# Half of an output projection as seven quadrant products in place of eight

## The chip, the cores and the metric

The kernel runs on one core of a Trainium2 chip, as one program with one launch. The metric is the device time of a whole execution in microseconds; lower is better. Every time below comes from runs on the chip or from one execution that the hardware profiler recorded.

## The reference

The program computes a model of two layers over 512 tokens of width 1024, in float32. Layer A mixes tokens by a gated spatial product in chunks of 128 and by attention to 256 memory rows; layer B by forgetting attention and by memory attention. Each layer then projects what it mixed, adds it to the residual after a norm, and runs a feed-forward of width 2816. Of layer A, with its output projection, the following is computed:

```python
proj = a @ w_in_a[layer]
u, v, q_mem = proj[..., :768], proj[..., 768:1536], proj[..., 1536:]
main = chunked_spatial_gating(u, v, w_s, b_s, ln_g, ln_b)     # gelu(u) * (w_s @ layernorm(gelu(v)) + b_s)
mixed = concatenate([main, memory_attention(q_mem, mem_n, w_mem_kv[layer])], axis=-1)   # 512 x 1024
h = h + rmsnorm(mixed @ w_out[layer], ln_mix_post[layer])
f = rmsnorm(h, ln_ffn_pre[layer])
f = (silu(f @ w_ffn_gate[layer]) * (f @ w_ffn_up[layer])) @ w_ffn_down[layer]
h = h + rmsnorm(f, ln_ffn_post[layer])
```

The change concerns `mixed @ w_out[0]`, a 512 x 1024 by 1024 x 1024 product.

## The kernel before

*Numbers in two parts.* Every float32 operand of a product is split into a high part (a cast to fp32r, on ScalarE, L276) and a low part (the operand less its high part, on VectorE, L277); `split` issues the pair. `mm3` (L217 to L221) then makes one product of three matmuls: high by high, high by low, low by high. So a product of 128 input rows with 512 columns costs three matmuls on TensorE, and each weight tile of 128 x 512 costs one operation on ScalarE and one on VectorE.

*Blocks.* The width of 1024 is eight blocks of 128. Blocks 0 to 5 of `mixed` are the six groups of the spatial product, 6 and 7 the two pairs of memory heads. `ORDER` (L40) takes them as 6, 7, 0, 1 and then 2, 3, 4, 5, since the first four are known earlier. The projection is cut accordingly into two halves of its inputs. `out_part` (L963) does the first: for each half of the output (`dh`) and each of four token blocks (`tb`), two pieces of two input blocks each; with the second piece the sum is copied out of PSUM to `ys[tb][dh]` by ScalarE (L982). In such a product 128 tokens of `mixed` are the stationary operand and 512 columns of weights the moving one. `mix_tail`, through `tail_of` (L877), does the second half: for each token block and output half, four input blocks in twelve matmuls, then an addition of `ys` (L904), the sum of squares (L917) and, per token block, the scaling by a power that POOL computes (L290, L944).

*The stage around it.* In `layer_a`, `attend` runs the four memory heads with pieces of other work between their steps. `join` (L446) puts two heads side by side and splits them into `mixed[6]` and `mixed[7]`. Then `gate_inputs(m)` (L793) makes the m-th block of `u`: 24 matmuls, a multiplication (L797) and a gelu (L798). `stats` and `normed(j)` make the normalized value rows and their parts. `spatial(g)` (L835) makes eight short matmuls into two PSUM tiles, four VectorE operations on them (L847, L850), a product with `us[g]` (L853) and, by `store`, the split into `mixed[g]`. The order is written out by hand: three `gate_inputs`, then `spatial(m - 3)` and `gate_inputs(m)` in turn for m = 3 to 5, then `spatial(g)` for g = 3 to 5, with 5, 5 and 6 of the sixteen pieces of `out_part` behind them. `queue` puts the loading of a block of weights three pieces ahead of its use.

*What orders the instructions.* Each engine runs its own list in order. A planner makes these lists: it goes through the program with its own estimate of durations and lets each engine take, of what it holds to be ready, what stands first in the program. Buffers are counted by tag: 36 tiles of 512 columns (`act`), 4 raw weight tiles, 8 high and 8 low weight parts, 4 temporaries, 6 of tag `p`, 3 PSUM tiles each of tags `mm` and `lg`, 2 of `tr`. An instruction that needs a tile is not ready before one is free. `behind` (L262) adds an order between two instructions by hand.

*Seven products.* The feed-forwards already use a form of Strassen's scheme. For a 2 x 2 block product, sums of the input blocks and of the weight blocks are formed, and seven products, summed in different ways, replace eight. `Down` (L1174) does so for the last matrix. Some of the sums of weights are made ahead, in DRAM: `sums_ahead` (L170) takes the next entry of `to_sum`, copies a block of weights to a DRAM tile by SP's queue and lets POOL's queue add another onto it (L190). `load` (L162) calls it for every second load while `credit[0]` is 0.5 (L857).

Of the kernel before, what the change touches and what calls it, by code (L numbers as in the profile page):

```python
# [43 lines left out]
def hybrid(ctx: ExitStack, tc: tile.TileContext, i: dict, out: bass.AP):  # L44
# [125 lines left out]
    def sums_ahead():  # L170

        if not to_sum:
            return
        w, layer, m = to_sum.pop(0)
        both = two_sums[w, layer, m] = dp.tile([P, 1040], F32, tag=name("sums"), name=name("sums"))[:, :1024]
        with behind(last_load[0]):
            if w == "w_down":
                four = both.rearrange("p (m k c) -> p m k c", m=4, k=2)  # L180
                for dh in range(2):
                    nc.sync.dma_start(four[:, :, dh, :],
                                      i[w][layer, 4 * dh : 4 * dh + 4, :, m, :].rearrange("m p c -> p m c"))
                more = i[w][layer, 4:8, :, m : m + 2, :].rearrange("m p k c -> p m (k c)")
                with behind(*(last_pow if m == 2 else ())):
                    G.dma_start(both.rearrange("p (m c) -> p m c", m=4), more, accum_op=ALU.add)
            else:
                nc.sync.dma_start(both.rearrange("p (a c) -> p a c", a=2),
                                  i[w][layer, m : m + 2, :, :512].rearrange("a p c -> p a c"))
                G.dma_start(both, i[w][layer, m + 1], accum_op=ALU.add)  # L190

    def moving_pair(src, aside=False):
# [4 lines left out]
        parts = []  # L197
# [6 lines left out]
    def out_weights(layer, kp, dh, aside=False):  # L204
        return moving_pair(i["w_out"][layer, 4 * dh : 4 * dh + 4, :, 256 * kp : 256 * kp + 256]
                           .rearrange("m p c -> p m c"), aside)

# [237 lines left out]

    def join(o, mixed, m, j):  # L446


        own, _ = rows(j)
        if j == 0:  # L450
            mixed[m] = act("mixedhi"), act("mixedlo")
# [41 lines left out]
    class MemHead(Softmax):  # L493
        def __init__(self, layer, pr, j, q, dst):
            super().__init__()
            self.kv, self.pr, self.j, self.q, self.dst = mem_kv[layer], pr, j, q[pr], dst
            self.blocks = (0, 1)
# [14 lines left out]
        def values(self, b):  # L512
# [5 lines left out]
            if b == 1:  # L518
                return join(self.o, self.dst, 6 + self.pr, self.j)

# [74 lines left out]

    def mem_heads(layer, q, mixed):
        heads = [MemHead(layer, pr, j, q, mixed) for pr in range(2) for j in range(2)]
        return heads


    def layer_a():
# [106 lines left out]
        with tc.tile_pool(name="sgu", bufs=1) as lp:  # L708
# [95 lines left out]
            attend(mem_heads(0, q, mixed), between=between)  # L804
            with behind(last_exp[0], last_turn[0]):
# [29 lines left out]
            def spatial(g):  # L835
# [17 lines left out]
                V.tensor_mul(t2, t.rearrange("p a b -> p (a b)"), us[g])  # L853
# [22 lines left out]

# [86 lines left out]
    def out_part(layer, mixed):  # L963
# [22 lines left out]
        return ys, [block(dh) for dh in range(2)]  # L986

    def mix_tail(layer, mixed, ys):
        attended = last_exp[0]

        def load(kp, dh, aside):
            with behind(attended):
                return out_weights(layer, 2 + kp, dh, aside)

        return tail_of([mixed[k] for k in ORDER[4:]], load, ys)

# [812 lines left out]
```

## Time and profile before

| | us |
|---|---|
| median of 3 runs | 1082.82 |
| lowest and highest run | 1082.56, 1083.18 |
| span of the profiled execution, first to last instruction | 1081.0 |
| median of the runs less this span | 1.8 |
| TensorE busy | 1073.2 |
| VectorE busy | 942.9 |
| ScalarE busy | 736.4 |
| POOL busy | 74.4 |

The profiled execution has no time of its own beside its span; what lies around the span is taken as the difference to the median of the runs. Engines are named PE (TensorE matmuls), PEld (its weight loads, which overlap with matmuls), DVE (VectorE), ACT (ScalarE), POOL (GpSimd) and SP (the queue that issues most transfers). A row of a timeline gives the start, the duration, the engine, the line of the kernel, the operation, output <- inputs, the shape and how many follow each other; in square brackets stands the idle time in front of it and what ended that. A row of windows gives for one stretch of the span each engine's busy time with its count of instructions.

### The profile page before, as it was taken

What the parts mean: (1) busy time and instruction counts of PE and PEld (TensorE: products, weight loads), DVE (VectorE), ACT (ScalarE), POOL (GpSimd) and SP (SyncE); (2) the same over time, 40 slices, a digit from 0 to 9 for tenths busy, and PEclk for the clock granted to TensorE, in tenths of its full rate; (3) what the DMA queues carried; (4) which work ended last, traced back from release to release, by engine and by line L of the source; (5) the groups of instructions that cost most, each with busy time, mean ns of one, the idle gap of its engine ahead of it and who ended that gap; (6) DMA issues with size and microseconds to landing.
All of it is one profiled execution on the core that took longest, in us unless ns stands there. A gap on an engine that the chain in (4) does not pass through costs nothing.

```text
span 1081.0 us, 20005 instructions
## 1 busy us (share of the span) xinstructions
PE 1073.2 (99%) x7234; PEld 982.1 (91%) x7234; DVE 942.9 (87%) x1894; ACT 736.4 (68%) x1605; POOL 74.4 (7%) x99
## 2 busy tenths in 40 slices
PE   9999999999999999999999999999999999999998
PEld 7998889999999988998988998889999999988996
DVE  8889659999989999996987899959999988999975
ACT  8776468666666667576765677858766666667564
POOL 0101001000000100000110111001000000000001
PEclk9999999999999999999999999999999999999999
DMA  7556666967665967264441754445977663646332
GB/s 275 167 136 180 190 157 204 255 186 194 172 169 149 300 177 230 92 206 126 128 128 48 208 128 115 126 123 171 255 199 194 162 158 115 176 128 206 112 118 79
DMA packets 131979, 179.52 MB, mean 166 GB/s; under 512 B 9964, under 2 KB 94200, under 8 KB 131880
## 3 DMA queue, kind: packets, MB, share of 16 engines
q1 hardware_dynamic: 119608, 160.53, 48.0%
q0 software_dynamic: 11712, 17.40, 10.3%
q8 instruction: 57, 0.93, 0.4%
q14 instruction: 42, 0.34, 0.1%
q10 hardware_dynamic: 560, 0.31, 0.1%
HBM read 158.71 MB, written 43.00 MB: 187 GB/s over the span
## 4 chain that ended last, share of the span: by engine, by line
PE 96%; ACT 2%; DVE 0%; issue 0%; DMA 0%; POOL 0%; POOLq 0%; ACTq 0%
PE a L219 7%; PE a L221 7%; PE a L220 7%; PE y L219 4%; PE y L220 4%; PE y L221 4%; PE ps L219 4%; PE ps L221 4%; PE ps L220 4%; PE e L219 4%; PE e L221 4%; PE e L220 3%; PE p L221 3%; PE p L219 3%; PE p L220 3%; PE x L219 3%
## 5 line engine op out<-in xcount | busy, mean ns | idle before, releaser
L276 ACT CAST whi<-raw 128x512 fp32r<-128x512 f32 x315 | 188.0, 618 | 59.8 <-PE a L220 12.9
L277 DVE TENSOR_TENSOR wlo<-raw,whi 128x512 fp32r<-128x512 f32 x315 | 210.2, 687 | 20.0 <-ACT whi L276 17.1
L219 PE MATMUL a<-xshi,whi 128*128 128x256 f32 x480 | 135.0, 281 | 0.0
L220 PE MATMUL a<-xslo,whi 128*128 128x256 f32 x480 | 134.9, 281 | 0.0
L221 PE MATMUL a<-xshi,wlo 128*128 128x256 f32 x480 | 134.7, 281 | 0.0
L276 ACT CAST whi<-room 128x512 fp32r<-128x512 f32 x160 | 98.1, 621 | 46.5 <-PE x L220 9.6
L277 DVE TENSOR_TENSOR wlo<-room,whi 128x512 fp32r<-128x512 f32 x160 | 108.9, 687 | 7.5 <-ACT whi L276 5.3
L219 PEld LDWEIGHTS a<-xshi,whi 128*128 128x128 f32 x480 | 90.3, 188 | 1.1 <-ACT e L1166 0.3
L220 PEld LDWEIGHTS a<-xslo,whi 128*128 128x128 f32 x480 | 90.4, 188 | 0.7
L221 PEld LDWEIGHTS a<-xshi,wlo 128*128 128x128 f32 x480 | 90.5, 189 | 0.0
L219 PE MATMUL ps<-xshi,whi 128*128 128x256 f32 x192 | 55.0, 289 | 0.1
L220 PE MATMUL ps<-xslo,whi 128*128 128x256 f32 x192 | 54.1, 283 | 0.0
L221 PE MATMUL ps<-xshi,wlo 128*128 128x256 f32 x192 | 54.0, 282 | 0.0
L276 ACT CAST ff<-u 128x256 fp32r<-128x256 f32 x80 | 32.3, 407 | 29.1 <-PE p L221 15.5
L219 PE MATMUL y<-whi,mixedhi 128*128 128x512 f32 x128 | 51.2, 400 | 0.0
L221 PE MATMUL p<-whi,ff 128*128 128x512 f32 x128 | 50.5, 395 | 0.0
L219 PE MATMUL p<-whi,ff 128*128 128x512 f32 x128 | 50.5, 395 | 0.0
L220 PE MATMUL y<-wlo,mixedhi 128*128 128x512 f32 x128 | 50.5, 395 | 0.0
L221 PE MATMUL y<-whi,mixedlo 128*128 128x512 f32 x128 | 50.4, 394 | 0.0
L220 PE MATMUL p<-wlo,ff 128*128 128x512 f32 x128 | 50.3, 393 | 0.0
L219 PE MATMUL x<-xshi,whi 128*128 128x256 f32 x160 | 45.1, 282 | 0.0
L220 PE MATMUL x<-xslo,whi 128*128 128x256 f32 x160 | 45.1, 282 | 0.0
(391 smaller groups left out, 3575.6 us busy)
## 6 DMA issues: line engine op xcount, KB each, us to landing
room<-in_w_up SPq DMA_DIRECT2D x36, 512.0 KB, 4.0
raw<-in_w_gate SPq DMA_DIRECT2D x24, 512.0 KB, 4.1
raw<-in_w_down SPq DMA_DIRECT2D x20, 512.0 KB, 4.5
sums<-in_w_gate SPq DMA_DIRECT2D x16, 512.0 KB, 5.8
sums<-in_w_gate POOLq DMA_DIRECT2D x16, 512.0 KB, 5.9
raw<-in_w_out SPq DMA_DIRECT2D x16, 512.0 KB, 3.5
sums<-in_w_down SPq DMA_DIRECT2D x32, 256.0 KB, 5.6
sums<-in_w_down POOLq DMA_DIRECT2D x16, 512.0 KB, 7.8
```

What stands on the lines that cost most here:

```text
L219: PE.matmul(o, w[0], x[0], start=start, stop=False, skip_group_check=more)
L220: PE.matmul(o, w[0], x[1], start=False, stop=False, skip_group_check=more)
L221: return PE.matmul(o, w[1], x[0], start=False, stop=stop, skip_group_check=more)
L276: last_hi[0] = A.copy(hi, src)
L277: last_split[0] = last_hi[0], (eng or V).tensor_sub(lo, src, hi)
```

## The change

The first half of layer A's projection is computed by a new class `OutPairs`, for two pairs `q` of input blocks: (6, 7) and (0, 1). In each pair, the inputs are two blocks by two halves of the tokens, and the weights two blocks by two halves of the output.

- `join` and `spatial` no longer split blocks 6, 7, 0 and 1: they hand them over whole (`pairs.whole`).
- `form` makes, per pair, sums of the four input quadrants (four VectorE operations of 256 columns) and their parts (three full splits and a half one).
- Per pair, two of the sums of weights are formed in DRAM by `sums_ahead`, which gets a branch for `w_out`, called twice among the memory heads. Two more are formed on VectorE (products 3 and 5).
- `pieces` runs products 0, 2, 3, 1, 4, 6, 5, each for both pairs, each with two token tiles of three matmuls. Their weights are split three pieces ahead. `tap` takes the running sums out of PSUM.
- Ten of the fourteen pieces (products 0, 2, 3, 1, 4) run 4, 2 and 4 behind the last three `spatial`; four (products 6, 5) run ahead of the tail's third token block.
- The second output half comes out with its sign turned in `ys`, which the tail undoes by subtracting.
- The tail's weights of layer A are loaded in two loads of 256 KB each into `act` tiles in place of one of 512 KB into a raw tile (`apart`).
- The eight gate sums of the feed-forward that were paced by loads (`credit[0] = 0.5`) are now called from `gate_inputs(1)` to `(5)` and from the last three `spatial`.

The core of the diff:

```diff
@@ sums_ahead
+            if w == "w_out":
+                four = both.rearrange("p (m k c) -> p m k c", m=4, k=2)
+                c = slice(256 * m, 256 * m + 128)
+                for dh in range(2):
+                    nc.sync.dma_start(four[:, :, dh, :],
+                                      i[w][layer, 4 * dh : 4 * dh + 4, :, c].rearrange("m p c -> p m c"))
+                more = i[w][layer, 4:8, :, 256 * m : 256 * m + 256].rearrange("m p c -> p m c")
+                G.dma_start(both.rearrange("p (m c) -> p m c", m=4), more, accum_op=ALU.add)
@@ moving_pair
+        if apart:
+            raws = [act("raw", F32).rearrange("p (m c) -> p m c", m=4) for _ in range(2)]
+            for x in range(2):
+                load(raws[x], src[:, :, x * P : x * P + P])
...
@@ join
-            return lambda: split(joined[m], *mixed[m])
+            return (lambda: whole(m, joined[m])) if whole else lambda: split(joined[m], *mixed[m])
@@ layer_a
             def gate_inputs(m):
                 gate_weights(m + 2)
+                if m:
+                    sums_ahead()
...
+            to_sum.extend(("w_out", 0, q) for q in range(2))
+            pairs = OutPairs(0)
+            between[1].append(sums_ahead)
+            between[2].append(sums_ahead)
...
-                store(t2, mixed, g)
+                if g < 2:
+                    pairs.whole(g, t2)
+                else:
+                    store(t2, mixed, g)
...
-            credit[0] = 0.5
...
-            ys, outs = out_part(0, mixed)
-            more = queue(outs)
             for m in range(3, NG):
                 spatial(m - 3)
                 gate_inputs(m)
+                if m == 3:
+                    pairs.forms(6)
+                elif m == 4:
+                    pairs.load_first()
+                    pairs.forms(0)
+            pairs.load_more()
+            begin, more = pairs.pieces()
+            begin()
             for g in range(3, NG):
                 spatial(g)
-                for f in take(more, 5 if g < NG - 1 else 6):
+                sums_ahead()
+                for f in take(more, 2 if g == 4 else 4):
                     f()
-        return mix_tail(0, mixed, ys)
+        tail, ys, tail_split = mix_tail(0, mixed, pairs.ys)
+
+        def mixed_tail(tb, *rest):
+            if tb == 2:
+                for f in more:
+                    f()
+            return tail(tb, *rest)
+
+        return mixed_tail, ys, tail_split
@@ OutPairs
+        ORDERED = (0, 2, 3, 1, 4, 6, 5)
...
+        def form(self, u0, u1):
+            t = temp("tsum")
+            one = act("mixedhi"), act("mixedlo")
+            split(u1, *one)
+            V.tensor_sub(t[:, left], u1[:, right], u0[:, right])
+            V.tensor_sub(u0[:, right], u0[:, left], u0[:, right])
+            V.scalar_tensor_tensor(out=t[:, right], in0=u0[:, right], scalar=-1.0, in1=u1[:, right],
+                                   op0=ALU.mult, op1=ALU.subtract)
+            zero = act("mixedhi"), act("mixedlo")
+            split(u0, *zero)
+            V.scalar_tensor_tensor(out=u1[:, left], in0=t[:, right], scalar=-1.0, in1=u1[:, left],
+                                   op0=ALU.mult, op1=ALU.subtract)
+            both, last = (flat(p()), flat(p())), p()
+            split(t, *both)
+            split(u1[:, left], last[:, 0], last[:, 1])
...
+        def weights(self, n, q):
+            r = self.raws[q]
+            if n == 3:
+                V.tensor_add(r["a11"], r["a21"], r["a11"])
+            elif n == 5:
+                V.tensor_add(r["a12"], r["a11"], r["a12"])
+            src = r[{0: "a11", 1: "s3", 2: "a12", 3: "a11", 4: "a22", 5: "a12", 6: "a21"}[n]]
+            w = pair_of_parts()
+            split(src, *(x.rearrange("p (m c) -> p m c", c=P) for x in w))
+            return w
+
+        def product(self, n, q, w):
+            bank = {0: "x", 3: "x", 6: "x", 5: "x", 2: "z", 1: "y", 4: "y"}[n]
+            first = n in (0, 2, 1)
+            if first and q == 0:
+                self.o[bank] = [ps("tr" if bank == "x" else "lg", s="y") for _ in range(2)]
+            for t in range(2):
+                x = self.pairs[q][n]
+                tokens = slice(t * P, (t + 1) * P)
+                mm3(self.o[bank][t], tuple(part[:, tokens] for part in x), w, first and q == 0, False, True)
+                if q:
+                    self.tap(n, t, self.o[bank][t])
+
+        def tap(self, n, t, o):
+            if n in (0, 3, 1):
+                kept = self.o[n, t] = act("kept", F32)
+                A.copy(kept, o)
+            elif n == 5:
+                ys[2 + t][0] = plain("y")
+                A.copy(ys[2 + t][0], o)
+            else:
+                tb, dh, of = {2: (t, 0, 0), 4: (t, 1, 3), 6: (2 + t, 1, 1)}[n]
+                ys[tb][dh] = plain("y")
+                V.tensor_add(ys[tb][dh], o, self.o[of, t])
+
+        def pieces(self):
+            order = [(n, q) for n in self.ORDERED for q in range(2)]
...
+            def run(x):
+                if x + 3 < len(order):
+                    ready[x + 3] = self.weights(*order[x + 3])
+                self.product(*order[x], ready.pop(x))
```

More of the change, by code (lines that the diff above doesn't have):

```diff
@@ L190, in sums_ahead, with moving_pair @@
                 G.dma_start(both, i[w][layer, m + 1], accum_op=ALU.add)
-    def moving_pair(src, aside=False):
+    def moving_pair(src, aside=False, apart=False):
+        parts = []
+        if apart:
+            raws = [act("raw", F32).rearrange("p (m c) -> p m c", m=4) for _ in range(2)]
+            for x in range(2):
+                load(raws[x], src[:, :, x * P : x * P + P])
+            for raw in raws:
+                hi, lo = (t.rearrange("p (m c) -> p m c", m=4) for t in pair_of_parts(aside=aside))
+                split(raw, hi, lo)
+                parts.append((hi, lo))
+            return parts
         raw = wp.tile([P, 1024], F32, tag="raw", name=name("raw"), bufs=4)
@@ L444, in hybrid, with join @@
     joined = {}
-    def join(o, mixed, m, j):
+    def join(o, mixed, m, j, whole=None):
         own, _ = rows(j)
         if j == 0:
-            mixed[m] = act("mixedhi"), act("mixedlo")
+            mixed[m] = None if whole else (act("mixedhi"), act("mixedlo"))
             f = joined[m] = temp("f", tag="acc", bufs=2)
@@ L493, in hybrid, with __init__ @@
     class MemHead(Softmax):
-        def __init__(self, layer, pr, j, q, dst):
+        def __init__(self, layer, pr, j, q, dst, whole):
             super().__init__()
+            self.whole = whole
             self.kv, self.pr, self.j, self.q, self.dst = mem_kv[layer], pr, j, q[pr], dst
@@ L594, in attend, with mem_heads @@
             f()
-    def mem_heads(layer, q, mixed):
-        heads = [MemHead(layer, pr, j, q, mixed) for pr in range(2) for j in range(2)]
+    def mem_heads(layer, q, mixed, whole=None):
+        heads = [MemHead(layer, pr, j, q, mixed, whole) for pr in range(2) for j in range(2)]
         return heads
@@ L803, in layer_a @@
             between[4] = [lambda k=k: gate_piece(k) for k in range(KT)]
-            attend(mem_heads(0, q, mixed), between=between)
+            attend(mem_heads(0, q, mixed, pairs.whole), between=between)
             with behind(last_exp[0], last_turn[0]):
@@ L992, in load @@
             with behind(attended):
-                return out_weights(layer, 2 + kp, dh, aside)
-        return tail_of([mixed[k] for k in ORDER[4:]], load, ys)
+                return out_weights(layer, 2 + kp, dh, aside, layer == 0)
+        return tail_of([mixed[k] for k in ORDER[4:]], load, ys, turned_sign=layer == 0)
     def boundary(phase, post, pre, nnorm, dst, block, evac, scaled=None):
```

44 lines of the change are left out of this document (39 added, 5 removed).

## The prediction

> **What bounds the kernel now.** I read the head of the page first, then the chain of waits, then tables of windows around the place of the change, and last the timelines of TensorE and VectorE inside them.
>
> ```profile
> span 1081.0 us, 20005 instructions
> PE 1073.2 (99%) x7234; PEld 982.1 (91%) x7234; DVE 942.9 (87%) x1894; ACT 736.4 (68%) x1605; POOL 74.4 (7%) x99
> PEclk9999999999999999999999999999999999999999
> PE 96%; ACT 2%; DVE 0%; issue 0%; DMA 0%; POOL 0%; POOLq 0%; ACTq 0%
> ```
>
> TensorE (PE) is 99% busy at full granted clock and is 96% of the chain that ended last. A matmul taken away anywhere is worth its own spacing, as long as what feeds the next ones keeps up. VectorE (DVE), at 87%, is the engine most likely not to.
>
> The change lies between the last softmax of layer A's memory heads, at about 83 us, and the end of the projection's tail, at about 163 us. The columns after the length of a stretch are busy times, with instruction counts in brackets, then clock, DMA share and GB/s.
>
> ```profile
> core 0: us, PE busy (x) PEld busy (x) DVE busy (x) ACT busy (x) POOL busy (x), PEclk, DMA share, GB/s
> 83.20:138.90 55.70, 55.70 (x266) 46.16 (x265) 44.79 (x92) 31.62 (x58) 5.45 (x6) 1.00 0.70 180
> 138.90:163.00 24.10, 24.10 (x115) 19.87 (x114) 11.44 (x22) 13.84 (x32) 2.49 (x4) 1.00 0.52 152
> 89.60:107.00 17.40, 17.40 (x85) 14.46 (x84) 16.92 (x34) 11.91 (x22) 0.87 (x1) 1.00 0.68 176
> ```
>
> TensorE has no idle time in any of these. VectorE has 55.7 - 44.8 = 10.9 us of room before the tail starts and 24.1 - 11.4 = 12.7 us within it, but it is not spread evenly: from 89.6 to 107 us it is 97% busy (16.92 of 17.40). So the stage has one saturated engine, and a second one that is saturated in its first third.
>
> **The change, part by part.** *TensorE.* The first half of the projection is now 2 halves of the output x 4 token blocks x 4 input blocks x 3 matmuls = 96 matmuls of 512 columns. Seven products x 2 pairs of input blocks x 2 token tiles x 3 = 84. What one costs is its spacing, not its duration, since they overlap:
>
> ```profile
> 130.49 0.47 PE L219 MATMUL y<-whi,mixedhi 128*128 128x512 f32 x1
> ...
> 138.23 0.39 PE L219 MATMUL y<-whi,mixedhi 128*128 128x512 f32 x1
> 138.70 0.39 PE L221 MATMUL y<-whi,mixedlo 128*128 128x512 f32 x1
> 138.93 0.40 PE L219 MATMUL y<-whi,mixedhi 128*128 128x512 f32 x1
> ```
>
> Between the first and the last row lie 36 matmuls, the last six of the sixteen pieces: 8.44 / 36 = 0.234 us each. Twelve fewer save 12 x 0.234 = 2.8 us, if TensorE never waits. The row at 138.93 is the first matmul of the tail. The Trainium skill ("TensorE: Matmul & The Clock Gate", section "Wait — 56ns, not 53.3ns?") puts warm N = 512 matmuls 215.7 ns apart; by that the saving would be 2.6 us, and the trace, 8% wider, decides.
>
> *VectorE, prices.* It works through queued 512-column operations at a spacing shorter than their duration:
>
> ```profile
> 99.09 0.68 DVE L277 TENSOR_TENSOR wlo<-raw,whi 128x512 fp32r<-128x512 f32 x1
> 99.69 0.69 DVE L853 TENSOR_TENSOR sgu<-s,u 128x512 f32<-128x512 f32 x1
> 100.29 1.29 DVE L277 TENSOR_TENSOR wlo<-raw,whi 128x512 fp32r<-128x512 f32 x2
> 101.49 0.69 DVE L277 TENSOR_TENSOR mixedlo<-sgu,mixedhi 128x512 fp32r<-128x512 f32 x1
> 225.87 0.42 DVE L1195 TENSOR_TENSOR t<-u,u 128x256 f32<-128x256 f32 x1
> 226.21 0.69 DVE L1131 TENSOR_TENSOR room<-room 128x512 f32<-128x512 f32 x1
> L1231 DVE TENSOR_TENSOR raw<-t,raw x8: 684/691/693, 361.3 to 966.8; 128x512 f32<-128x512 f32 x8
> 141.91 0.69 DVE L904 TENSOR_TENSOR y<-y,y 128x512 f32<-128x512 f32 x1 [0.95 <-PE y L221]
> ```
>
> The first four rows start 0.60 us apart, so 0.60 is the price of any 512-column one: a split's low part, a sum of weights (the feed-forward's own is L1231, 0.69 long as well), or an addition out of PSUM (L904, the same length). A 256-column sum, 0.42 long, gives way to the next after 0.34.
>
> *VectorE, count.* Added: two calls that form the sums of the inputs, each with three full splits, one half split and four 256-column sums, 3 x 0.60 + 5 x 0.34 = 3.5, together 7.0. Fourteen weight splits, 8.4. Four weight sums (products 3 and 5, for both pairs), 2.4. Six additions out of PSUM (products 2, 4 and 6, two token tiles each), 3.6. That is 21.4. Removed: eight weight splits and four splits of mixed 6, 7, 0 and 1, 12 x 0.60 = 7.2. Net +14.2 us, against 10.9 + 12.7 = 23.6 us of room, which shrinks by the 2.8 that TensorE gains. It fits in sum; the question is when.
>
> The Trainium skill ("VectorE: DVE Perf Modes", section "Terms") says that a drain after each operation holds the next one until the pipe is empty, so that a 512-column operation would cost its whole 0.69 us. By that the net would be 24 operations' worth x 0.69 = 16.3 us and the forecast below about 2 us worse; the 0.60 us starts above do not bear it out for operations that don't depend on each other.
>
> *VectorE, when.* Ten of the fourteen pieces run before the tail. By then TensorE has 60 matmuls behind it in place of 96, so in program order it would ask for the tail after 55.7 - 36 x 0.234 = 47.3 us. VectorE has until then: the 44.8 of before, + 7.0 for the forms, + 13 splits (three pieces ahead of the tenth) 7.8, + 3 sums 1.8, + 4 additions (products 2 and 4) 2.4, - 11 splits 6.6 (the twelfth removed one, of mixed 6, was before 83 us) = 57.2. Of this the last seven of the tail's eight weight splits need not be there when the tail starts: each one feeds 3 matmuls, 0.70 us, and takes 0.60. 57.2 - 7 x 0.60 = 53.0 us. At the 97% of the saturated stretch it is 54.6. TensorE's work ends 5.7 to 7.3 us before VectorE's. The four pieces left over are 24 x 0.234 = 5.6 us of work whose weights, but for the fourteenth's split and sum (1.2 us), are ready by then. They stand in the third token block in the text, but the planner orders each engine by what is ready, and their priority is only a little lower; I take it that most of them fill the gap. What is left is 5.7 - 5.6 = 0.1 to 7.3 - 5.6 + 1.2 = 2.9 us of waiting, and the gain 2.7 to -0.1. I take 1.3, the middle.
>
> Within the tail VectorE has 12.7 us of room and 1.2 to 2.4 us of extra work (product 6's additions, what is left of product 5's weights); that hides there, and without that cover it would cost its own length before the boundary.
>
> *Edits costed at nothing.* ScalarE: each split brings a cast, each stored product a copy; +6 casts for weights, +4 net for forms at 0.5 and the same eight copies, some 5 us on an engine with 55.7 - 31.6 = 24 us of room in the stage. The sign turned in the second half of the output is the same subtraction in L904's place. Loads: the two input sums of weights made in DRAM (four SP transfers and two POOL ones more), four loads of 512 KB as before, two more of 256 KB, and the tail's four loads cut into eight. They are covered by lead:
>
> ```profile
> 80.32 0.38 SPq L164 DMA_DIRECT2D raw<-in_w_out  x1
> 80.75 0.56 SPq L188 DMA_DIRECT2D sums<-in_w_gate  x1
> 87.96 5.92 SPq L164 DMA_DIRECT2D raw<-in_w_out  x2
> ...
> raw<-in_w_out SPq DMA_DIRECT2D x16, 512.0 KB, 3.5
> sums<-in_w_gate POOLq DMA_DIRECT2D x16, 512.0 KB, 5.9
> ```
>
> The first load for the projection goes out at 80.3 us, 34 us ahead of its first matmul, and lands in 3.5; the stage's DMA share of 0.70 leaves room for some 2.5 MB more. If that lead were gone, a load would cost its 3.5 to 5.9 us once. Taking away the pacing of the gate sums (half a credit a load) and calling them by hand leaves all eight in the same stage; they only have to be there for the feed-forward, after 163 us.
>
> *What waits.* Product 6's addition must read its bank before product 5 writes it, with 0.70 us of the other token tile between: 0.69 plus a queue of one or two operations, 0 to 1.2 us, inside the range above. The bank pair that the chain holds through the tail's first half is one that the tail doesn't use until it turns the rows, after its third block.
>
> **The rivals.** *Everything is hidden* (full gain). If VectorE's forms get into the small gaps before 89 us, and the last spatial products' parts are asked for later than I count, there is no wait: 1082.8 - 2.8 = 1080.0. For it: the room of 23.6 against 14.2. Against it: 97% busy from 89.6 to 107, just where the forms come.
>
> *VectorE becomes the bound, in program order* (slower). If the planner does not pull the last four pieces forward, TensorE stands still before the tail's first matmul for the 5.7 to 7.3 us; the four pieces later find VectorE ready and cost their own time. Net 5.7 - 2.8 = 2.9 to 7.3 - 2.8 = 4.5, so 1082.8 + 3.7 = 1086.5. It decides as soon as VectorE's backlog at the tenth piece exceeds 2.8 us and nothing is put in the gap. For it: the order of the text, and in the trace of before TensorE runs these pieces and the spatial products in strict program order (114.75 to 138.93). Against it: there it had no reason to do otherwise.
>
> *POOL's queue.* Its accumulating transfer waits in order for SP's two halves, and behind it the power that normalizes the value rows:
>
> ```profile
> 86.15 0.81 POOL L190 DMA_DIRECT2D sums<-in_w_gate  x1 [19.45 <-DMA sums<-in_w_gate]
> 88.16 1.34 POOL L290 TENSOR_TENSOR rv<-rv,mhalf 128x4 f32<-128x4 f32 x1 [1.20 <-DVE rv L815]
> ```
>
> If a sum called by hand lands in front of that power and is 5.9 us late, the value splits and the first spatial product are late by as much, less about 1 us of slack: 5.9 - 1 - 2.8 = +2.1 on top of the forms' pressure, about 1085. For it: the calls now stand beside it. Against it: the power is called earlier than the first gate sum. That the change makes fewer matmuls than it says is not possible: 84 for 96 is counted from the loops.
>
> **How the numbers follow.** Spans and runs differ by 1082.8 - 1081.0 = 1.8 us; I take the difference as unchanged. Forecast: 1082.8 - 1.3 = 1081.5 us (span 1079.7), chance 0.50, its own range 1080.1 to 1082.9. All hidden, 1080.0: 0.22. Program order, 1086.5: 0.24. POOL, 1085: 0.04. Noise of a few tenths puts the low end at 1079.7; the high end, 1086.9, takes in most of the program-order case. 0.2%, 2.2 us, is about what a measurement of this kernel can tell from no change, so the bounds are 1080.65 and 1084.99. Faster: 0.22 and the lowest fifth of the forecast's range, 0.10: 0.32. Slower: 0.24 + 0.04 = 0.28. Same: 0.40.
>
> **What would show it.** Right: 84 matmuls of 512 columns at 0.234 us, VectorE 95% busy or more from 90 us to past 135 us, pieces of the last two products ahead of or among the first two token blocks' matmuls, and one to three short waits of TensorE for a weight's low part (L277) between 115 and 140 us. Wrong: no such wait and the first feed-forward matmul 2.8 us earlier (all hidden); one wait of 5 us or more before the tail's first matmul, with the last four pieces behind the second token block (program order); or a wait that ends on a load or on POOL. Waits in the boundary after the tail, where I count none, would break the sum as well.

## The result, and the profile after

The changed kernel takes 1090.55 us, median of 4 runs (1089.7 to 1091.11), beside 1083.0 us before (1082.56 to 1083.31): a ratio of 1.0068, 95% interval 1.0056 to 1.008. It is slower by some 7.5 us, and the forecast of 1081.5 us and its range up to 1086.9 us are missed on the slow side. The profiled execution has a span of 1088.0 us, 7.0 more than before. Its page begins so, with the line of the chain of waits last:

```profile
span 1088.0 us, 20048 instructions
PE 1074.6 (99%) x7222; PEld 981.7 (90%) x7222; DVE 956.6 (88%) x1922; ACT 740.9 (68%) x1615; POOL 76.6 (7%) x101
...
PE 90%; DVE 4%; ACT 3%; DMA 2%; issue 1%; POOL 0%; SPq 0%; POOLq 0%; ACTq 0%
```

The twelve matmuls are gone (7234 to 7222), and yet TensorE's busy time rose from 1073.2 to 1074.6 us. TensorE's share of the chain fell from 96% to 90%; VectorE, ScalarE and DMA now hold 9%. To see where, here is the stage from the first spatial matmul behind the forms to the last four transposes in the tail, before and after (columns as in the prediction: window, length, busy times, clock, DMA share, GB/s):

```profile
94.44:162.33 67.89, 67.89 (x326) 56.28 (x325) 45.24 (x84) 36.50 (x72) 5.80 (x8) 1.00 0.66 178
```

```profile
94.69:168.43 73.74, 68.88 (x313) 56.20 (x312) 59.38 (x113) 41.78 (x82) 4.98 (x7) 0.95 0.58 157
```

The stage is 5.85 us longer. Of that 73.74 - 68.88 = 4.86 us is TensorE idle, where it had none. But its busy time, too, is 1.0 us more, where 2.8 less was due. Beside e11 below, in which nothing waits and this busy time is 65.53 us, 68.88 - 65.53 = 3.35 us are matmuls that ran slower, at a mean granted clock of 0.95. The other 1.15 us of the 7.0 lie outside the stage (further below).

The idle time is two waits, 1.93 + 2.93 us. TensorE's timeline:

```profile
123.56 0.50 PE L236 MATMUL y<-whi,ff 128*128 128x512 f32 x1 [1.93 <-ACT kept L1118]
...
140.41 0.97 PE L236 MATMUL y<-whi,mixedhi 128*128 128x512 f32 x3 [2.93 <-ACT whi L293]
...
142.29 0.63 PE L236 MATMUL y<-whi,mixedhi 128*128 128x512 f32 x1
142.72 0.63 PE L237 MATMUL y<-wlo,mixedhi 128*128 128x512 f32 x1
...
145.10 0.39 PE L237 MATMUL y<-wlo,mixedhi 128*128 128x512 f32 x1
145.33 0.39 PE L238 MATMUL y<-whi,mixedlo 128*128 128x512 f32 x1
```

Behind the second wait the matmuls start 0.43 us apart (142.29 to 142.72) until 144.85, and only then 0.23 again. Behind the first one the same is seen in windows of 2 us; the number ahead of the DMA share is the granted clock:

```profile
122.00:124.00 2.00, 0.44 (x2) 0.40 (x3) 2.00 (x4) 1.98 (x5) 0.00 (x0) 1.00 0.99 195
124.00:126.00 2.00, 2.00 (x7) 1.55 (x6) 2.00 (x6) 1.71 (x4) 0.00 (x0) 0.60 0.37 72
126.00:128.00 2.00, 2.00 (x6) 1.55 (x5) 2.00 (x5) 0.76 (x2) 0.00 (x0) 0.55 0.00 0
128.00:130.00 2.00, 2.00 (x14) 1.82 (x13) 1.66 (x4) 1.29 (x3) 0.00 (x0) 1.00 0.00 0
```

So a wait here costs more than its length. Behind each of the two, twelve matmuls take 4.45 us (123.56 to 128.01 and 140.41 to 144.85) in place of the 2.8 at 0.233 us each: 4.86 us of waiting brought 2 x 1.65 = 3.3 us of slow matmuls.

What each wait ended on is read from ScalarE's timeline and SP's, the last fence being SP's of before:

```profile
119.72 0.62 ACT L293 CAST whi<-raw 128x512 fp32r<-128x512 f32 x1 [1.82 <-DVE raw L1092]
120.72 1.14 ACT L293 CAST whi<-raw 128x512 fp32r<-128x512 f32 x2 [0.37 <-DVE raw L1092]
121.76 0.61 ACT L293 CAST mixedhi<-sgu 128x512 fp32r<-128x512 f32 x1
...
122.92 1.07 ACT L1118 COPY kept<-y 128x512 f32<-128x512 f32 x2
...
139.74 0.62 ACT L293 CAST whi<-raw 128x512 fp32r<-128x512 f32 x1 [4.92 <-DMA raw<-in_w_out]
```

```profile
132.14 0.35 SPq L164 DMA_DIRECT2D raw<-in_w_gate  x1
133.34 0.34 SPq L164 DMA_DIRECT2D raw<-in_w_up  x1
133.77 5.95 SPq L164 DMA_DIRECT2D raw<-in_w_out  x6
```

```profile
126.36 0.37 SPq L164 DMA_DIRECT2D raw<-in_w_out  x1
128.17 0.34 SPq L164 DMA_DIRECT2D raw<-in_w_gate  x1
```

*The first wait.* Product 3 writes the bank of product 0, so it waits for product 0's copy (L1118). On ScalarE that copy stands behind the casts of product 3's own weights, and these wait for VectorE's sums (L1092). VectorE is 100% busy ahead of it (10.00 of 10 us from 110 to 120).

*The second wait.* The tail's weights are loaded only from 133.77 us on. SP takes its transfers in order, and ahead of them stand the feed-forward's first loads, which had to wait for a raw tile until VectorE had split what was in it: they leave at 132.14 and 133.34 us, 0.07 us behind the ends of two splits (131.39 and 132.59, 0.68 long). In before the last of the tail's loads left at 126.36 us, ahead of the feed-forward's first. The first of the tail's casts comes 6.0 us after its load was issued.

*Outside the stage.* Two rows of each kernel show the memory heads, which the change touches by the transfers issued there and by the splits of blocks 6 and 7 that it leaves out; the first two rows are of before, the others of after:

```profile
48.38 0.28 PE L505 MATMUL mlg<-memk,q 128*128 128x256 f32 x1
...
94.44 0.28 PE L844 MATMUL s<-whi,vhi 128*128 128x256 f32 x1
```

```profile
47.97 0.28 PE L523 MATMUL mlg<-memk,q 128*128 128x256 f32 x1
...
94.69 0.28 PE L868 MATMUL s<-whi,vhi 128*128 128x256 f32 x1
...
689.74 0.64 PE L553 MATMUL lg<-ka,qa 128*128 128x512 f32 x2 [0.74 <-DMA ka<-whi]
```

After is 0.41 us ahead at the first of the heads' matmuls and 0.25 us late at the first spatial one: 0.66 us lost between. From the stage's end to the end of the span it takes 919.6 us in place of 918.7, with a wait of 0.74 us in layer B that before did not have. So 7.0 = -0.41 + 0.66 + 5.85 + 0.9. These are differences of two single executions. Over the thirteen changed kernels the first matmul of the heads stands anywhere from 47.97 to 50.04 us, and what follows the stage takes 918.1 to 919.6 us, so the -0.41 and the 0.9 lie within what one execution differs from another. The 0.66 does not: between those two rows all thirteen take 46.70 to 46.81 us, beside 46.06 before.

### The profile page after: what moved, and what is told of

The parts are those of the page before. It is cut to its first block, busy times and chain, and to the rows that moved or that the text cites. A ratio compares the mean times of both kernels' runs of the same rounds, so it can differ in the third digit from the quotient of the medians.

```text
span 1088.0 us, 20048 instructions
## 1 busy us (share of the span) xinstructions
PE 1074.6 (99%) x7222; PEld 981.7 (90%) x7222; DVE 956.6 (88%) x1922; ACT 740.9 (68%) x1615; POOL 76.6 (7%) x101
## 4 chain that ended last, share of the span: by engine, by line
PE 90%; DVE 4%; ACT 3%; DMA 2%; issue 1%; POOL 0%; SPq 0%; POOLq 0%; ACTq 0%
PE a L237 7%; PE a L238 7%; PE a L236 7%; PE e L237 3%; PE e L236 3%; PE e L238 3%; PE y L236 3%; PE y L237 3%; PE y L238 3%; PE ps L238 3%; PE ps L236 3%; PE ps L237 3%; PE p L238 3%; PE p L236 3%; PE p L237 3%; PE x L237 3%
## 5 line engine op out<-in xcount | busy, mean ns | idle before, releaser
L293 ACT CAST whi<-raw 128x512 fp32r<-128x512 f32 x319 | 190.4, 618 | 62.4 <-PE a L237 12.9
L294 DVE TENSOR_TENSOR wlo<-raw,whi 128x512 fp32r<-128x512 f32 x319 | 212.8, 686 | 21.4 <-ACT whi L293 18.5
L294 DVE TENSOR_TENSOR wlo<-room,whi 128x512 fp32r<-128x512 f32 x160 | 108.7, 686 | 6.7 <-ACT whi L293 4.7
L236 PE MATMUL y<-whi,mixedhi 128*128 128x512 f32 x112 | 44.7, 406 | 2.9 <-ACT whi L293 2.9
L237 PE MATMUL a<-d2lo,whi 128*128 128x256 f32 x160 | 45.0, 281 | 0.0
L238 PE MATMUL a<-d2hi,wlo 128*128 128x256 f32 x160 | 45.0, 281 | 0.0
L237 PE MATMUL e<-t3lo,whi 128*128 128x256 f32 x160 | 44.9, 281 | 0.0
```

Of the source, the lines that this page charges most:

```text
L236: PE.matmul(o, w[0], x[0], start=start, stop=False, skip_group_check=more)
L237: PE.matmul(o, w[0], x[1], start=False, stop=False, skip_group_check=more)
L238: return PE.matmul(o, w[1], x[0], start=False, stop=stop, skip_group_check=more)
L293: last_hi[0] = A.copy(hi, src)
L294: last_split[0] = last_hi[0], (eng or V).tensor_sub(lo, src, hi)
```

## The experiments

The theory at the start: two orders cause it, that of SP's loads (A) and that of ScalarE's copies (B), each with slow matmuls behind its wait. Its rival: VectorE's backlog stands behind both, and would show elsewhere once the orders are mended. All times are medians with the ratio to before and its 95% interval; before took 1082.8 to 1083.3 us beside them. "Stage" and "idle" are those of TensorE in the profiled execution, from the first spatial matmul to the last four transposes in the tail, as above. A profiled execution can lie up to 1.8 us from the median of its kernel (e4), so stages and idle times are compared rather than spans.

| kernel | time us | ratio | stage us | idle us |
|---|---|---|---|---|
| before | 1082.8 | 1 | 67.9 | 0 |
| after | 1090.55 | 1.0068 (1.0056 to 1.008) | 73.7 | 4.9 |
| e1 tail's loads first | 1086.70 | 1.0034 (1.0022 to 1.0046) | 69.9 | 2.6 |
| e2 copies first | 1089.93 | 1.0064 (1.0051 to 1.0076) | 72.5 | 5.0 |
| e3 both | 1085.99 | 1.0029 (1.0019 to 1.0039) | 69.4 | 3.3 |
| e4 raw tiles for the tail | 1085.75 | 1.0023 (1.0014 to 1.0033) | 69.6 | 1.9 |
| e5 e3, sums on POOL | 1088.55 | 1.0052 (1.004 to 1.0065) | 72.2 | 4.5 |
| e6 e4 and copies first | 1084.89 | 1.0017 (1.0008 to 1.0026) | 68.8 | 2.6 |
| e7 e3 without the sums | 1083.61 | 1.0006 (0.9997 to 1.0014) | 67.5 | 1.7 |
| e8 e6, sums on POOL | 1087.66 | 1.0041 (1.0027 to 1.0055) | 70.6 | 4.0 |
| e9 e6, product 6 ahead of 4 | 1084.65 | 1.0012 (1.0003 to 1.0021) | 68.3 | 2.1 |
| e10 e9, additions later | 1084.63 | 1.0015 (1.0006 to 1.0024) | 68.9 | 1.9 |
| e11 e1 without the sums | 1082.03 | 0.9995 (0.9986 to 1.0003) | 65.6 | 0.1 |
| e12 e1 without the weight sums | 1084.90 | 1.0015 (1.0006 to 1.0024) | 68.0 | 2.0 |

### The two orders: e1, e2, e3

*e1* lets the feed-forward's loads stand behind the tail's:

```diff
-                tail_split[0] = last_split[0]
+                tail_split[0] = last_split[0] + ((last_load[0],) if loads_first else ())
...
```

> One edge of order is added: on SP's queue the feed-forward's first weight loads stand behind the tail's eight loads of the projection. Theory A (two separate waits, each made by an order of instructions: at 121.4 us TensorE waits 1.9 us for the copies of product 0, which stand behind casts on ScalarE; at 137.5 us it waits 2.9 us for the tail's first weights, whose loads stand on SP behind a feed-forward load that waits for a raw tile; and each wait is followed by 8 to 10 matmuls at 0.43 us in place of 0.233): the second wait and its slow matmuls go, 2.9 + 10 x 0.195 = 4.9 us, so about 1085.6 us, and the tail's first load goes out before 125 us. Rival B (VectorE's backlog is the bound, the order of loads only shows it): TensorE waits for low parts of weights in the same place instead, 1089 to 1090.5 us.

It took 1086.7 us, 3.85 less than after. Its loads on SP, and what TensorE still waits for:

```profile
113.47 16.00 SPq L164 DMA_DIRECT2D raw<-in_w_out  x8
```

```profile
123.56 0.50 PE L236 MATMUL y<-whi,ff 128*128 128x512 f32 x1 [1.87 <-ACT kept L1118]
138.86 0.50 PE L237 MATMUL y<-wlo,mixedhi 128*128 128x512 f32 x1 [0.68 <-DVE wlo L294]
```

The loads leave 20 us earlier, and the wait for them is gone; one of 0.68 us for VectorE takes its place. The order of the loads is so shown to be worth half of the loss. Theory A expected 1085.6 us and the rival 1089 or more; A is nearer, but the wait in its place is the one that the rival named.

*e2* puts product 0's copies ahead of product 3's casts on ScalarE, and the split of block 3 behind them; in every piece, too, the split of the weights three pieces ahead now stands behind the product and not ahead of it:

```diff
-                if x + 3 < len(order):
-                    ready[x + 3] = self.weights(*order[x + 3])
                 self.product(*order[x], ready.pop(x))
+                if x + 3 < len(order):
+                    with behind(*(copies if order[x + 3][0] == 3 and x else ())):
+                        ready[x + 3] = self.weights(*order[x + 3])
...
```

> In place of splitting weights ahead of a piece's product, the split comes behind it; the casts of product 3's weights and the split of mixed 3 stand behind the copies of product 0 on ScalarE. Theory A: the wait at 121.4 us and its slow matmuls go (1.9 + 8 x 0.19 = 3.5 us), but the loads still leave when VectorE splits product 6's weights at about 131 us, so most of it comes back as a longer wait before the tail: 1088 to 1090.5 us. If the two waits were independent of each other: 1087. Rival B: TensorE waits at the same place for weights of product 3, same time as the changed kernel, 1090.5.

It took 1089.93 us, which is not to be told from after. The wait for the copy is gone, and 1.11 us for the emptying of a spatial bank (L874) and 1.52 us for a low part (L294), both on VectorE, came in its place. The wait for the tail's loads stays, 2.38 us at 139.52, with slow matmuls behind it.

*e3* has both edits.

> Both orders of the two experiments beside it. Theory A: 4.9 + 3.5 us go, 1090.55 - 8.4 = 1082.1 us, with waits of TensorE under 0.5 us between 115 and 150 us and no slow matmuls. Rival B: VectorE's work is the same, so waits of several us stay, 1088 to 1090.

It took 1085.99 us, 3.9 more than the theory of the two orders expected. Both waits are gone, but three others stand there, and all end on VectorE:

```profile
126.95 0.35 PE L868 MATMUL s<-whi,vhi 128*128 128x256 f32 x1 [1.10 <-DVE s L874]
132.42 0.50 PE L237 MATMUL y<-wlo,mixedhi 128*128 128x512 f32 x1 [1.51 <-DVE wlo L294]
139.15 0.50 PE L237 MATMUL y<-wlo,mixedhi 128*128 128x512 f32 x1 [0.68 <-DVE wlo L294]
```

None of them is followed by slow matmuls. The rival is now the theory: behind the orders stands VectorE's backlog.

### Raw tiles for the tail: e4, e6

*e4* loads the tail's weights as before the change, four loads of 512 KB in place of eight of 256 KB:

```diff
-                return out_weights(layer, 2 + kp, dh, aside, layer == 0)
+                return out_weights(layer, 2 + kp, dh, aside)
```

> One part of the change undone: the tail's weights are loaded as before, four loads of 512 KB into raw tiles. Theory A: they stand ahead of the feed-forward's loads on SP, but wait for raw tiles that products 6 and 5 hold until 131 to 140 us, so the wait before or within the tail grows: 1092 to 1096 us. Rival C (loads in rows of 512 bytes are what is late): 1085 to 1088 us.

1085.75 us: the first theory, which called the loads late in this form as well, expected 1092 to 1096 and fell here. SP's timeline and TensorE's:

```profile
134.15 7.19 SPq L164 DMA_DIRECT2D raw<-in_w_out  x4
142.18 0.34 SPq L164 DMA_DIRECT2D raw<-in_w_gate  x1
```

```profile
125.57 0.59 PE L236 MATMUL y<-whi,ff 128*128 128x512 f32 x1 [1.86 <-ACT kept L1118]
```

```profile
137.80 1.14 ACT L293 CAST whi<-raw 128x512 fp32r<-128x512 f32 x2 [0.97 <-DMA raw<-in_w_out]
```

In this execution everything in the stage stands 2.0 us later than in after (the wait for the copy ends at 125.57 in place of 123.56 us). Set against TensorE's work, the loads therefore leave 1.6 us earlier than in after, at the place where the feed-forward's first load left there, and the feed-forward's stand behind them. The first cast of what they bring comes 3.65 us after the issue in place of 5.97, and the wait is gone. So some 4 us are won, 1.6 of them by the moment of issue and 2.3 by a faster landing. Rival C's time was met; but whether the loads land faster by their form or by what no longer stands ahead of them was not tried apart.

*e6* adds the order of the copies to e4.

> The tail's weights loaded as four loads of 512 KB through raw tiles, as before the change, and product 0's copies ahead of product 3's casts. The run with raw tiles alone (1085.75 us) had one wait left, 1.86 us for a copy, with some 1.6 us of slow matmuls behind it. Theory A (each wait has its own cause and they add): both go, about 1082.3 us. Rival B (VectorE's backlog stands behind the copy): the wait comes back on VectorE's low parts, as with both orders, at 1.1 + 1.5 + 0.7 us; about 1085 us.

1084.89 us, beside 1082.3 for causes that add and 1085 for the backlog. The waits are the first two of e3, 1.10 us for L874 at 127.0 and 1.51 us for L294 at 132.47.

### Relief for VectorE: e5, e8 and e7, e11, e12

*e5* is e3 with the four weight sums on POOL; *e8* is e6 with the same edit:

```diff
-                V.tensor_add(r["a11"], r["a21"], r["a11"])
+                G.tensor_add(r["a11"], r["a21"], r["a11"])
...
-                V.tensor_add(r["a12"], r["a11"], r["a12"])
+                G.tensor_add(r["a12"], r["a11"], r["a12"])
```

> Both orders of the run before (the tail's loads ahead of the feed-forward's, product 0's copies ahead of product 3's casts), and the four weight sums of products 3 and 5 made by POOL instead of VectorE. What is left of TensorE's waiting in that run, 1.10 + 1.51 + 0.68 = 3.3 us, ended on VectorE each time. Theory (VectorE's backlog sets these waits): four sums less are 4 x 0.60 = 2.4 us less of backlog, so the waits shrink to about 1 us and the time from 1086.0 to about 1083.6. Rival (POOL is slow at it, or later): the casts that need the sums come later than with VectorE, TensorE waits for ScalarE's cast of product 3 or 5 instead, and the time stays at 1086 or rises by a few us.

> The tail's weights through raw tiles, product 0's copies ahead of product 3's casts, and the four weight sums on POOL. Theory (VectorE's backlog is the last bound): between 1080.5 and 1083, the lowest of the changed kernels that compute the whole result. Rival (POOL is slow at it): a wait for the cast of product 3 or 5, 1085 us or more.

Both became slower, 1085.99 to 1088.55 and 1084.89 to 1087.66 us. The waits of TensorE still end on VectorE, and VectorE's and POOL's timelines in e5 show why:

```profile
107.24 0.68 DVE L294 TENSOR_TENSOR wlo<-raw,whi 128x512 fp32r<-128x512 f32 x1
108.24 1.65 DVE L294 TENSOR_TENSOR wlo<-raw,whi 128x512 fp32r<-128x512 f32 x1
111.35 2.31 DVE L294 TENSOR_TENSOR mixedlo<-sgu,mixedhi 128x512 fp32r<-128x512 f32 x1
118.35 1.68 DVE L294 TENSOR_TENSOR wlo<-raw,whi 128x512 fp32r<-128x512 f32 x1
```

```profile
108.06 1.27 POOL L1099 TENSOR_TENSOR raw<-raw,raw 128x512 f32<-128x512 f32 x1 [18.00 <-DVE wlo L294]
111.56 1.54 POOL L1099 TENSOR_TENSOR raw<-raw,raw 128x512 f32<-128x512 f32 x1
118.20 1.27 POOL L1101 TENSOR_TENSOR raw<-raw 128x512 f32<-128x512 f32 x1 [5.10 <-DVE wlo L294]
```

Beside three of POOL's four sums a split takes 1.65 to 2.31 us in place of 0.68, and each of these splits ends 0.56 us behind the end of POOL's sum, even the one that began 0.21 us ahead of it. The fourth sum, at 120.19 us, runs beside operations that read PSUM, and stretches a split by no more than 0.1 us. So three of the sums cost VectorE 1.0 to 1.6 us each, more than the 0.60 of making them. The Trainium skill ("SBUF — State Buffer", section "Who interferes with whom") states that a VectorE instruction with two inputs in SBUF contends with a GpSimd instruction that reads SBUF, and calls the ports that they share an exclusive lock. The trace agrees, by the 0.56 us. VectorE's busy time in the stage did not fall: 59.31 us in e3 and 60.81 in e5, 59.52 in e6 and 59.79 in e8. So these two runs did not relieve VectorE, and are no test of the theory; the rival's time came, but not its waits for a cast.

*e7* is e3 without VectorE's new sums (four of 512 columns and eight of 256), so it leaves out a part of the result.

> Both orders, and VectorE's new sums left out: the four weight sums of products 3 and 5 and the eight 256-column sums that form the products' inputs, so that another result is computed; splits, matmuls, copies, additions and loads are all there. VectorE has 4 x 0.60 + 8 x 0.34 = 5.1 us less to do in the stage. Theory (VectorE's backlog): the 3.3 us of waits that both orders leave are gone, and the time is 1086.0 - 3.3 = 1082.7, down to 1080.5 if the matmuls saved come out in full. Rival (an order or a dependency, not the load): waits of 2 to 3 us stay, 1085 to 1086 us.

1083.61 us: 2.4 less than e3, and idle time 1.7 in place of 3.3. VectorE itself stood idle now, for ScalarE; the rows are VectorE's, then ScalarE's:

```profile
120.01 0.69 DVE L294 TENSOR_TENSOR wlo<-raw,whi 128x512 fp32r<-128x512 f32 x1 [1.54 <-ACT whi L293]
```

```profile
118.19 1.27 ACT L1115 COPY kept<-y 128x512 f32<-128x512 f32 x2 [1.59 <-PE y L238]
119.35 0.62 ACT L293 CAST whi<-raw 128x512 fp32r<-128x512 f32 x1
```

Product 3's casts were held behind the copies, and these behind TensorE: without the sums that order is a loss. *e11* drops it; it is e1 without the sums.

> The tail's loads first and VectorE's new sums left out (four weight sums, eight 256-column sums; another result is computed), but without the order that puts product 0's copies ahead of product 3's casts. With that order the run without sums kept waits of 1.00 + 0.68 us, while VectorE itself stood idle for 1.54 us at 118.5 for ScalarE's cast of product 3, which was held behind the copies. Theory (what is left there is ScalarE's order, not VectorE's load): without it VectorE runs on, the waits fall below 1 us together, and the time to 1082.0 to 1082.7 from 1083.6. Rival: the copies fall behind casts again, a wait of about 1.9 us for a copy with slow matmuls after it, 1086 to 1087 us as with the tail's loads first alone.

1082.03 us, as expected. The stage of e1 and that of e11:

```profile
94.75:164.63 69.88, 67.33 (x313) 55.02 (x312) 59.44 (x114) 42.15 (x84) 4.98 (x7) 0.98 0.62 166
```

```profile
95.29:160.91 65.62, 65.53 (x313) 53.71 (x312) 53.75 (x102) 41.59 (x83) 4.98 (x7) 1.00 0.65 177
```

With VectorE's busy time down from 59.44 to 53.75 us, TensorE's idle time falls from 2.55 to 0.09 us and the clock stays at 1.00, with the order of copies and casts as in after. The first wait, too, is thus VectorE's.

*e12* leaves out the weight sums alone.

> The tail's loads first, and only the four weight sums of products 3 and 5 left out (another result is computed); the eight 256-column sums of the inputs stay. Between 1086.7 us (all sums in, waits of 1.87 us for a copy and 0.68 us for a low part, and slow matmuls after the first) and 1082.03 us (no sums at all, no waits). Theory (the link decides: product 3's casts wait for VectorE's sums, and product 0's copies stand behind them on ScalarE): the link is cut, so the 1.87 us wait and the slow matmuls behind it (about 1.6 us) go, 1086.7 - 3.5 = 1083.2; the low part's 0.7 us may stay. Rival (only the amount of VectorE's work counts): 2.4 of the 5.1 us are taken off, so about half of the 4.7 us come back, 1084.5, and waits on VectorE's low parts or on its emptying of the spatial bank are left.

1084.9 us: near the rival's 1084.5 and not the 1083.2 of the link from sum to cast to copy. The longer of the two waits is still for the copy, which is late now behind another cast that waits for VectorE (ScalarE's timeline, then TensorE's):

```profile
121.47 0.62 ACT L293 CAST mixedhi<-sgu 128x512 fp32r<-128x512 f32 x1 [0.98 <-DVE sgu L877]
...
122.63 1.08 ACT L1114 COPY kept<-y 128x512 f32<-128x512 f32 x2
```

```profile
123.27 0.50 PE L236 MATMUL y<-whi,ff 128*128 128x512 f32 x1 [1.22 <-ACT kept L1114]
```

So the loss shrinks with VectorE's work: 2.4 us off VectorE gives 1086.7 - 1084.9 = 1.8 us, 5.1 off give 4.7. It does not shrink in proportion. TensorE's idle time falls from 2.55 us only to 2.02 in e12, and to 0.09 in e11; 1.3 of e12's 1.8 us are busy time (67.33 to 66.02 us), because the wait for the copy, now 1.22 us, is no longer followed by slow matmuls. That the rival's number came out is in part luck.

### VectorE's order: e9, e10

*e9* is e6 with product 6 ahead of product 4, all twelve pieces ahead of the tail; *e10* also holds product 2's additions behind the last spatial product's split.

```diff
-        ORDERED = (0, 2, 3, 1, 4, 6, 5)
+        ORDERED = (0, 2, 3, 1, 6, 4, 5)
...
-                for f in take(more, 2 if g == 4 else 4):
+                for n, f in enumerate(take(more, (4, 2, 6)[g - 3])):
... (e10)
+                add = lambda: V.tensor_add(ys[tb][dh], o, self.o[of, t])
+                if n == 2:
+                    self.late.append(add)
...
```

> The kernel with raw tiles and copies first (1084.89 us; waits of 1.10 us at 127.0 and 1.51 us at 132.47), and in it product 6's pieces written ahead of product 4's, both ahead of the tail. In that run TensorE already takes product 6 first (at 130.33), while VectorE splits product 4's weights first (128.36 and 130.75) and product 6's low part comes at 131.74. Theory (the 1.51 us wait is a matter of VectorE's order at that place): it goes, 1084.9 - 1.5 = 1083.4. Rival (VectorE is simply behind by that much, whatever it does first): the wait moves to another low part or to the tail's weights, 1084.5 to 1085.5.

> The same, and product 2's two additions held until the last spatial product's parts are made. Before, they stand (123.79, 1.2 us) in front of the four operations that empty the spatial product's bank, for which TensorE waited 1.10 us at 127.0. Theory: that wait goes too, 1083.4 - 1.1 = 1082.3. Rival (VectorE's backlog as a whole): the wait is met again at the next low part, no gain over the run with the order of 6 and 4 alone.

1084.65 and 1084.63 us, not to be told from e6's 1084.89: the rival held both times. The waits that were aimed at went (1.51 us in e9, 1.1 in e10), and others of 0.5 to 1.3 us came, for a copy that stands on ScalarE behind a cast that waits for VectorE's L877. Another order only changed what met the backlog.

No version that computes the whole result is faster than before; the best, e9 and e10, are 0.1% slower. Even e11, which makes none of VectorE's new sums and waits for almost nothing, can't be told from before (0.9986 to 1.0003): its stage is 2.3 us shorter, but 0.75 us of that go in the memory heads.

## Why the prediction was wrong, step by step

The forecast span was 1079.7 us and the measured one is 1088.0, 8.3 more. Of these, 4.86 - 1.5 = 3.36 us are waits beyond those in the sum, 3.35 matmuls that ran slower behind the waits, 0.44 a smaller saving of matmuls, and 1.15 lie outside the stage.

*TensorE, 2.8 us: nearly right.* Where nothing waits (e11), the stage's busy time is 67.89 - 65.53 = 2.36 us less.

*VectorE's prices and count: right.* In the stage its busy time rose by 59.38 - 45.24 = 14.1 us, and over the whole execution by 956.6 - 942.9 = 13.7, where 14.2 were counted; its 28 more instructions are the 40 added and 12 removed of the count.

*When, 0.1 to 2.9 us of waiting, taken as 1.3 of gain:* the engine was right, the middle of the range low and the place wrong. The planner did pull product 6 ahead of the tail, and still 2.6 us (e6) to 3.3 us (e3) of waits remain with the orders mended. The sign that the text named, one to three short waits for a weight's low part, is not in after; it appears in e3, as 1.51 and 0.68 us. The windows of after (VectorE is the third busy time):

```profile
90.00:100.00 10.00, 10.00 (x48) 8.25 (x48) 9.19 (x20) 9.64 (x19) 0.00 (x0) 1.00 0.06 24
...
110.00:120.00 10.00, 10.00 (x49) 8.30 (x48) 10.00 (x23) 3.56 (x7) 2.83 (x4) 1.00 1.06 261
120.00:130.00 10.00, 8.07 (x37) 6.66 (x36) 9.65 (x19) 7.36 (x14) 0.00 (x0) 0.83 0.49 90
130.00:140.00 10.00, 7.48 (x33) 5.59 (x31) 7.66 (x14) 2.37 (x5) 0.00 (x0) 1.00 0.65 194
```

VectorE is 92% busy from 90 to 100 us and saturated to about 130, but not 95% to 135: from 130 to 140 it is 77%, as TensorE, kept waiting, fed it less. The sum treated VectorE as one queue with a due time at the tail; in fact each spatial bank, copy and low part has a due time of its own.

*What a wait costs: missing.* The sum took every wait at its length. Two of 1.93 and 2.93 us were each followed by matmuls at nearly half the rate, 1.65 us lost behind each, 3.3 in all.

*"Edits costed at nothing", the step that failed.* "Loads ... are covered by lead" argued from the first load at 80.3 us. The tail's eight loads have no such lead: they left SP from 133.77 us on, behind feed-forward loads that waited for VectorE. The text even had the price, "a load would cost its 3.5 to 5.9 us once", and the run paid 3.85 (after less e1). That the two agree is luck: the 3.85 are a wait of 2.93 us and 1.65 us of slow matmuls, less the 0.68 that e1 still waits there. The "2.5 MB" of room in that passage does not follow from its rows either: a share of 0.70 at 180 GB/s leaves some 4.3 MB in 55.7 us. Nothing else rests on it, and the queue's order cost the time, not its share. ScalarE's "24 us of room" was true on average, and no help: it works in order, and the copies that TensorE waited for stood behind casts that waited for VectorE.

*The heads and layer B: not counted.* The memory heads take 0.64 to 0.75 us longer in every changed kernel. In after it is busy time of TensorE at a clock of 1.00 (46.57 beside 45.97 us) and not a wait; which part of the change brings it is open. Behind the stage twelve of the thirteen changed kernels have a wait of 0.5 to 1.3 us in layer B (L553), in most of them for a transfer; e6 and before have none. Why is open, and so is its cost, since the time behind the stage lies on both sides of before's 918.7 us. With these, e3's 3.2 us over before are about accounted for: 1.5 in the stage, 0.66 in the heads, 0.4 behind the stage, and 0.5 by which its heads began later, which is within what such executions differ by.

*Rivals.* VectorE as the bound was the right side, but not as put: no wait of 5.7 us ahead of the tail, since product 6's pieces were pulled forward, and the 2.93 us there ended on a load. POOL held nothing up. Product 6's addition before product 5 cost no wait. The prediction named "a wait that ends on a load" as what would prove it wrong, and that is the longest of the two.

## What to carry to other kernels

Trading matmuls for additions pays only where the adding engine has room at that very place: 12 matmuls of 0.23 us were bought with 14 us on an engine that was already 97% busy at the start of the stage. Work "off the path" has to be checked in each in-order queue it enters (SP's, ScalarE's) for what stands ahead of it and what that waits for; lead shown for the first transfer says nothing of the last. On TensorE, a wait of some 2 us costs more than its length: here about 1.6 us on top of it.

## What the hardware showed

*The clock.* In the fourteen traces, an idle stretch of 1.86, 1.87, 1.93, 1.94, 2.38 or 2.93 us within the stage was followed, within about 1 us of the work resuming, by a granted clock of 0.50 (windows of 1 us) for 3 to 3.6 us, in which 512-column matmuls start 0.43 us apart, a further loss of about 1.6 us; none of up to 1.52 us was. The Trainium skill ("TensorE: Matmul & The Clock Gate", section "Why this matters for your kernels") warns of idle gaps over about 3 us. Here under 2 us are enough, and the measurement decides; the half rate and the length of the slow stretch agree with its Part 1.

*VectorE and POOL.* An addition on POOL stretched a VectorE split beside it from 0.68 to as much as 2.31 us (e5), and the split ended 0.56 us behind the addition each time.
